# A hybrid decoder layer: operands made in pairs, the value unit moved back, and the convolution tail placed inside the output projection

## The chip, the cores and the metric

The kernel runs on one core of a Trainium2 chip. The metric is the device time of one execution in microseconds (us). Five engines work beside each other, each on its own queue: TensorE (PE: matmuls, and PEld: its weight loads), VectorE (DVE), ScalarE (ACT), GpSimd (POOL) and SyncE (SP), which issues most of the DMA transfers.

## The reference

One decoder layer over 2048 tokens of 1024 channels, in float32. A joint projection gives queries, keys and values for sliding-window attention, and the input of a gated convolution group; both outputs are joined and projected, and a SwiGLU feed-forward part follows. Cut to what matters:

```python
hn = rms_norm(x, mix_pre_g)
proj = hn @ w_in                       # q (8 heads), k and v (2 heads each), a and gate
attn = sliding_window_attention(q, k, v, attn_sinks, rel_bias)   # window 128, T5 bias, sinks
g = a * sigmoid(gate)                  # 512 channels
g = causal_depthwise_conv(g, conv_dw, width=31) + conv_dw_b
conv = silu(layer_norm(g, conv_ln_g, conv_ln_b)) @ w_conv_pw
h = x + rms_norm(concat([attn, conv]) @ w_out, mix_post_g)
hn = rms_norm(h, ffn_pre_g)
out = h + rms_norm((silu(hn @ w_gate) * (hn @ w_up)) @ w_down, ffn_post_g)
```

## The kernel before

The 2048 tokens are worked in four tiles of 512 (tile 0 to tile 3). Every float32 matmul operand is split into a high part (a copy rounded for the matmul, made by ACT) and a low part (the difference, made by DVE), and each product is three matmuls: high by high, high by low, low by high.

**A0 to A3 (`stage_a`)** project one token tile each: 14 units of 128 output channels, 24 matmuls each. Units 0 to 7 are the gates and inputs of the convolution group; then come K (unit 8), V (unit 9) and four query blocks q0 to q3. Results lie in four PSUM banks named `mm` until ACT or DVE copies or splits them. K goes to `kz`, V is transposed on PE and copied to `vtok`, the queries go to four `ql` tiles. `kz`, `vtok` and `ql` exist once, so a tile's K, V and queries overwrite what the attention of the tile before still reads. After each unit `step(i)` runs a hook, if there is one. The hooks prepare the next tile: `h1` loads its x, `h0` reads rows of x for the row norms, `h2` and `h3` make and spread the row scale (`gb`), and `h4` and `h5` each make four of the eight `hn` operands (`split_x`: a scaled product on DVE, a copy on ACT, a subtraction on DVE).

**B0 to B3 (`stage_b`)** are the attention of a tile, four blocks of 128 queries. `front(b)` makes the scores (PE from `ql` and `kz`, then masking, bias and maximum on DVE, exponentials on ACT); `back(b)` scales them, transposes them and makes the weighted sum with `vtok`. The order is front 0, front 1, back 0, front 2, back 1, front 3, back 2, back 3. They use three banks named `tr`.

**C0 to C3** are the convolution: 31 taps a block on DVE (`stage_taps`, tile `fc`), and a tail (`stage_tail`, `conv_tail`) that transposes, normalises over the channels, transposes back and applies the swish. The tail writes four 128x512 blocks to `mixT` in memory, as the attention does with its own four. **J** multiplies the pointwise convolution weights into the output weights. **W0 to W3 (`stage_w`)** read `mixT` for a tile, two channel blocks at a time (`gi` = 0 to 3; 0 and 1 are attention, 2 and 3 convolution), split them and multiply by the output weights; `norm_w` follows. **H, F and G** are the feed-forward part: sums of operands, up and gate products, down products.

The order of the work is written by generators. A main generator yields a cost after each piece; each yield pumps the lanes (`lb` attention, `lc` taps, `lw` output projections, `ld` join and tails of tiles 0 and 1, `lh` and others), which emit pieces at a set rate per unit of main cost. `lane.until(name)` emits the rest of a named item at once. A planner then orders the instructions of each engine by priority, which follows the order of emission (the taps stand back a little), and by when its own timeline has them ready. In tile 0 and tile 1 the hooks before are:

```python
hooks = {2: h1, 4: h0, 8: h2, 10: h3, 11: h4, 12: h5}   # t == 0
hooks = {0: h1, 2: h0, 7: h2, 9: h3, 10: h4, 11: h5}    # t == 1
```

Ahead of K, `before_kv()` emits all that is left of the attention of the tile before. Tiles 2 and 3 have their tails and output projections in lane `lw`, which runs beside the first down projection (G0): C2, W2, C3 (once tile 3's taps are done), W3.

Of the kernel before, what the change touches and what calls it, by code (L numbers as in the profile page):

```python
# [12 lines left out]
F32 = mybir.dt.float32  # L13
# [5 lines left out]
ALU = mybir.AluOpType  # L19
# [18 lines left out]
def layer_kernel(ctx, tc, x, xT, cols, rows, sinks, relb, onehot, w_in, w_four, w_pw, w_out, w_gate, w_up, w_down, out):  # L38
# [22 lines left out]
    def f2(tag, shape=(P, T)):  # L61
        return t_(tag, shape)
# [263 lines left out]
            hn.append(hk)  # L326
        return hn

    def stage_a(t, hn, before_kv, hooks, post=None):
        L = f"A{t}"  # L330
        lab[0] = L
        rb = None
# [54 lines left out]
        for c in range(4):  # L387
# [13 lines left out]
            half.send(proj(2 * c + 1, tr if post and c == 2 else mm))  # L401
            yield 5.2
            step(2 * c + 1)
        before_kv()
        lab[0] = L
        ok = proj(8)
        if t:
# [6 lines left out]
        vtt(kz[:, 1, P:], ok, kz[:, 0, P:].bitcast(F32), ALU.subtract)  # L414
        yield 5.2
        step(8)
        ov = proj(9)
        vt = f2("fa")
        if post:
            vtt(vt, ov, rb, ALU.mult)  # L420
        else:
            act(vt, ov, AF.Copy)
        yield 5.2
        step(9)
        q = []
        for i in range(4):
            oq = proj(10 + i)
            if i == 0:
                pv = mm()
                for s in range(4):  # L430
                    nc.tensor.transpose(pv[:, s * P : (s + 1) * P], vt[:, s * P : (s + 1) * P], ident)
                if t:
                    nc.vector.tensor_copy(vtok[:, 0], vtok[:, 4])
                nc.vector.tensor_copy(vtok[:, 1:5].rearrange("p a b -> p (a b)"), pv)
            qi = hl("ql")
            if post:
                qt = f2("fa")
                stt(qt, oq, 0.125, rb, ALU.mult, ALU.mult)
                act(qi[:, 0], qt, AF.Copy)
                vtt(qi[:, 1], qt, qi[:, 0].bitcast(F32), ALU.subtract)  # L440
            else:
                act(qi[:, 0], oq, AF.Copy, scale=0.125)
                stt(qi[:, 1], oq, 0.125, qi[:, 0].bitcast(F32), ALU.mult, ALU.subtract)
            q.append(qi)
            yield 5.2
            step(10 + i)
        qs[t] = q

    done_ = []
# [1 line left out]
    def stage_b(t):  # L451
# [115 lines left out]
            yield 1.8  # L567

        live = {}
        for b in range(5):  # L570
            if b < 4:
                yield from front(b)
            else:
                yield YC
            if b:
                yield from back(b - 1)

    def conv_in(t, c):
        g = t_("glu", (P, 576))[:, 0 : HALO + T]
# [29 lines left out]
            nc.sync.dma_start(y_scr[c, :, t * T : (t + 1) * T], y)  # L609
            yield 0.68  # L610

    def stage_tail(t):
        L = f"C{t}"
        lab[0] = L
        yt = t_("yt", (P, 4, 4 * P))
        ycs = []
        turn = turner(yt, ycs)
        for c in range(4):
            lab[0] = L
            y = f2("fc")  # L620
            nc.sync.dma_start(y, y_scr[c, :, t * T : (t + 1) * T])
            ycs.append(y)
            turn(c)
            yield 0.5
        yield from conv_tail(t, yt)

    def conv_tail(t, yt):
        L = f"C{t}"
        lab[0] = L
        mv = sm(8).rearrange("p (s a) -> p s a", a=2)  # L630
        for s in range(4):
            st = sm(6)
            nc.vector.bn_stats(st, yt[:, s])
            nc.vector.bn_aggr(mv[:, s], st)
        r = rsqrt(mv[:, :, 1], 4, 1.0)
        nmr = sm(4)
        stt(nmr, mv[:, :, 0], -1.0, r, ALU.mult, ALU.mult)
        yield YL if t < 2 else YL2
        lab[0] = L
        for s in range(4):  # L640
            act(yt[:, s], yt[:, s], AF.Identity, scale=r[:, s : s + 1], bias=nmr[:, s : s + 1])
        for c in range(4):
            b = ct()
            for s in range(4):
                nc.tensor.transpose(b[:, s * P : (s + 1) * P], yt[:, s, c * P : (c + 1) * P], ident)
            th = f2("fc")
            act(th, b, AF.Tanh, scale=lnh[:, c : c + 1], bias=lnh[:, 4 + c : 5 + c])
            v = f2("fc")
            act(v, b, AF.Identity, scale=ln_g[:, c : c + 1], bias=ln_b[:, c : c + 1])
            stt(v, th, 1.0, v, ALU.add, ALU.mult)  # L650
            nc.sync.dma_start(mixT[4 + c, :, t * T : (t + 1) * T], v)
            yield 2
            lab[0] = L

# [108 lines left out]
    def stage_w(w, spill, G, atag, htag, mtag, bank_of, norm=None):  # L763
        L = f"W{w}"
        lab[0] = L
        acc = [f4(atag) for _ in range(4)]

        def acts(gi, ms=None):
            aa = []
            for m in ms or load(gi):  # L770
                a = hl(htag)
                act(a[:, 0], m, AF.Copy)
                vtt(a[:, 1], m, a[:, 0].bitcast(F32), ALU.subtract)
                aa.append([a])
            return aa

        stage = spare_tile() if w == 1 else None

# [12 lines left out]
            lab[0] = L  # L791
        nxt = acts(0, first)
        for gi in range(KC // G):
            aa = nxt
            for n in range(2):
                lab[0] = L
                if n == 0 and gi + 1 < KC // G:
                    if w < 2 and G * gi + G == 4:
                        ld.until(f"C{w}")
                        lab[0] = L  # L800
                    rows_next = load(gi + 1)
                if n == 1 and gi + 1 < KC // G:
# [5 lines left out]
        tail = norm_w(w, spill, acc, mtag, gb)  # L808
        if norm:
            norm(tail)  # L810
        else:
            yield from tail

    def norm_w(w, spill, acc, mtag, gb):
        L = f"W{w}"
# [640 lines left out]
    for t in range(NT):  # L1456
        hooks = {}
        if t + 1 < NT:
# [7 lines left out]
            def h4(t=t + 1):  # L1466
                hn_a[t] = split_x(t, xa[t][0], xa[t][2], range(4))

            def h5(t=t + 1):
                hn_a[t] += split_x(t, xa[t][0], xa[t][2], range(4, KC))  # L1470

            def h0(t=t + 1):
                row_norms([t] if t == 1 else [2, 3], "p" if t == 1 else "hl")
# [3 lines left out]
                next(xa[t][2])  # L1477

            if t == 0:
                hooks = {2: h1, 4: h0, 8: h2, 10: h3, 11: h4, 12: h5}  # L1480
            elif t == 1:
                hooks = {0: h1, 2: h0, 7: h2, 9: h3, 10: h4, 11: h5}
            else:
                hooks = {H1: h1, H2: h2, H3: h3, H4: h4}
        run(mark(stage_a(t, hn_a[t], (lambda: lb.until(f"B{t-1}")) if t else (lambda: None), hooks,
                         None if t else norm_x(0, x0, sum_squares(0, x0))), f"A{t}"))
        lb.add(f"B{t}", stage_b(t))
        if t == 2:
            hn_a[t + 1] += split_x(t + 1, xa[t + 1][0], xa[t + 1][2], range(4, KC))
    lw.until("W0")  # L1490
# [14 lines left out]
    lc.until("T2")  # L1505
    lc.rates["T3"] = RC3
    ws, ops = (2, 3), {}
    lw.add("C2", stage_tail(2))
    lw.add("W2", stage_w(2, True, 2, "mid", "ql", "at", tr))
    lw.add("C3", stage_tail(3), lambda: since(lc, "T3", CS))  # L1510
    lw.add("W3", stage_w(3, True, 2, "mid", "ql", "at", tr, norm=lambda g: lw.add("N3", g)))
    lw.add("B11.2", stage_h_plain(ws, ops, "B11", 0))
    run(stage_p2((0, 1), mids[0], td))
    lw.until("N3")
# [70 lines left out]
```

## Time and profile before

| | |
|---|---|
| three timed runs, median (lowest to highest) | 1944.02 us (1936.79 to 1946.71) |
| the profiled execution, its own time | 1941.57 us |
| its span, first to last instruction | 1939.8 us |
| granted TensorE clock, mean | 0.993 |
| DMA traffic | 443.55 MB, mean 229 GB/s |

A row of the timeline begins with the start and the length in us, then the engine, the line, the operation and "output<-inputs". A tile's name carries the stage after an @: `mm@A` is an `mm` bank used by an A stage, `ql@W` a `ql` tile used by W. Most DVE instructions have the line of a helper, L85. In brackets stand the idle time of the engine before the row's first instruction and what ended it. In a table by stage each engine has its busy time and, in brackets, its number of instructions.

### The profile page before, as it was taken

What the parts mean: (1) busy time and instruction counts of PE and PEld (TensorE: products, weight loads), DVE (VectorE), ACT (ScalarE), POOL (GpSimd) and SP (SyncE); (2) the same over time, 40 slices, a digit from 0 to 9 for tenths busy, and PEclk for the clock granted to TensorE, in tenths of its full rate; (3) what the DMA queues carried; (4) which work ended last, traced back from release to release, by engine and by line L of the source; (5) the groups of instructions that cost most, each with busy time, mean ns of one, the idle gap of its engine ahead of it and who ended that gap; (6) DMA issues with size and microseconds to landing.
All of it is one profiled execution on the core that took longest, in us unless ns stands there. A gap on an engine that the chain in (4) does not pass through costs nothing.

```text
span 1939.8 us, 26752 instructions
## 1 busy us (share of the span) xinstructions
PE 1896.2 (98%) x8714; PEld 1537.5 (79%) x8714; DVE 1488.1 (77%) x2760; ACT 968.7 (50%) x1911; POOL 209.5 (11%) x311
## 2 busy tenths in 40 slices
PE   9998999999999999999999999999999999999998
PEld 7876776777678888877888788878888888888886
DVE  6998999988785999988988775778666665455557
ACT  5454444656667534333445466576533443345443
POOL 2010011221010000000000010010032332311000
PEclk9999999999999999999999999999999999999999
DMA  9876756678868776688397779589644442376654
GB/s 330 297 276 194 254 162 192 203 236 310 260 213 292 232 250 224 222 279 275 126 320 227 258 267 321 184 313 355 211 163 154 163 158 101 131 247 190 211 191 156
DMA packets 230011, 443.55 MB, mean 229 GB/s; under 512 B 22984, under 2 KB 49008, under 8 KB 229872
## 3 DMA queue, kind: packets, MB, share of 16 engines
q1 hardware_dynamic: 208560, 407.24, 63.1%
q10 hardware_dynamic: 19392, 28.32, 4.0%
q0 software_dynamic: 1920, 6.29, 0.8%
q8 instruction: 68, 1.11, 0.2%
q14 instruction: 71, 0.58, 0.1%
HBM read 320.64 MB, written 121.12 MB: 228 GB/s over the span
## 4 chain that ended last, share of the span: by engine, by line
PE 70%; DVE 16%; DMA 9%; issue 2%; ACT 2%; POOL 1%; SPq 0%; DVEq 0%; ACTq 0%; POOLq 0%
PE mm@F L108 37%; PE mm@G L108 19%; DVE fc@C L85 7%; PE mm@A L108 4%; PE tr@W L108 4%; PE mm@W L108 3%; PE tr@B L108 1%; DMA glu@C<-glu_scr 1%; DMA mixT<-fc@C 1%; DMA td<-fc@G 1%; DVE x@A L85 1%; DMA p@X<-w_four 1%; DMA p@A<-x 1%; DVE p@B L490 1%; DMA mids<-fa@F 1%
## 5 line engine op out<-in xcount | busy, mean ns | idle before, releaser
L85 DVE SCALAR_TENSOR_TENSOR fc@C<-glu@C,colt,fc@C 128x512 f32<-128x512 f32 x480 | 351.5, 751 | 1.7
L108 PE MATMUL mm@F<-hl@H,w@F 128*128 128x512 f32 x1056 | 254.3, 389 | 0.0
L108 PEld LDWEIGHTS mm@F<-hl@H,w@F 128*128 128x128 f32 x1056 | 197.9, 188 | 41.0
L108 PE MATMUL mm@G<-hl@G,hl@G 128*128 128x512 f32 x924 | 224.8, 393 | 2.6 <-DVE x@G L85 1.8
L864 ACT ACTIVATE w@F<-chl@F 128x512 fp32r<-128x512 f32 x220 | 135.5, 625 | 144.4 <-PE mm@F L108 138.6
L108 PEld LDWEIGHTS mm@G<-hl@G,hl@G 128*128 128x128 f32 x924 | 172.3, 188 | 39.0 <-ACT hl@G L864 3.4
L108 PE MATMUL mm@G<-w@G,hl@G 128*128 128x512 f32 x876 | 199.5, 389 | 0.0
L108 PE MATMUL mm@A<-hl@A,w@A 128*128 128x512 f32 x792 | 191.5, 394 | 1.2 <-DVE w@A L85 1.2
L108 PEld LDWEIGHTS mm@G<-w@G,hl@G 128*128 128x128 f32 x876 | 164.5, 188 | 34.1
L108 PEld LDWEIGHTS mm@A<-hl@A,w@A 128*128 128x128 f32 x792 | 147.4, 188 | 34.1 <-issue 1.7
L85 DVE TENSOR_TENSOR w@F<-chl@F,w@F 128x512 fp32r<-128x512 f32 x198 | 147.1, 747 | 35.7 <-ACT w@F L864 35.2
L108 PE MATMUL mm@F<-mid@H,w@F 128*128 128x512 f32 x528 | 131.7, 392 | 2.9 <-DVE fa@F L85 2.9
L108 PE MATMUL mm@F<-ql@H,w@F 128*128 128x512 f32 x528 | 130.2, 391 | 2.0 <-ACT w@F L864 1.6
L108 PE MATMUL mm@F<-p@H,w@F 128*128 128x512 f32 x528 | 129.0, 389 | 0.0
L108 PE MATMUL mm@F<-x@H,w@F 128*128 128x512 f32 x528 | 128.0, 391 | 0.0
L108 PEld LDWEIGHTS mm@F<-mid@H,w@F 128*128 128x128 f32 x528 | 99.6, 189 | 24.0 <-DVE fa@F L85 3.3
L108 PEld LDWEIGHTS mm@F<-ql@H,w@F 128*128 128x128 f32 x528 | 98.5, 188 | 23.3 <-ACT w@F L864 2.2
L108 PEld LDWEIGHTS mm@F<-x@H,w@F 128*128 128x128 f32 x528 | 98.7, 188 | 22.0 <-DVE sm@B L85 0.8
L108 PEld LDWEIGHTS mm@F<-p@H,w@F 128*128 128x128 f32 x528 | 99.1, 188 | 20.7 <-ACT at@F L1122 0.2
L85 DVE TENSOR_TENSOR w@G<-raw@G,w@G 128x512 fp32r<-128x512 f32 x73 | 50.4, 691 | 67.5 <-ACT w@G L864 66.6
L108 PE MATMUL mm@W<-w@W,hl@W 128*128 128x512 f32 x384 | 97.9, 401 | 4.2 <-ACT mid@W L745 1.9
L133 ACT ACTIVATE w@A<-raw@A 128x512 fp32r<-128x512 f32 x104 | 63.5, 625 | 75.1 <-PE mm@A L108 43.6
(310 smaller groups left out, 3194.1 us busy)
## 6 DMA issues: line engine op xcount, KB each, us to landing
mids<-fa@F SPq DMA_DIRECT2D x154, 256.0 KB, 2.7
raw@A<-w_in SPq DMA_DIRECT2D x52, 512.0 KB, 4.7
w@A<-lo_in SPq DMA_DIRECT2D x84, 256.0 KB, 3.8
fc@G<-mids SPq DMA_DIRECT2D x77, 256.0 KB, 3.4
fa@G<-mids SPq DMA_DIRECT2D x75, 256.0 KB, 5.1
w@W<-lo_out SPq DMA_DIRECT2D x48, 256.0 KB, 5.0
chl@F<-w_gate SPq DMA_DIRECT2D x22, 512.0 KB, 4.0
raw@F<-w_gate SPq DMA_DIRECT2D x22, 512.0 KB, 3.9
```

The source lines that it names most:

```text
L85: r = op(*args, **kw)
L108: r = nc.tensor.matmul(*args, **kw)
L133: act(w[:, 0], raw, AF.Copy)
L490: read = nc.vector.tensor_tensor_reduce(out=pr[:, h], in0=os[g][:, j, P:], in1=bias[0][:, h], op0=ALU.add, op1=ALU.max, scale=1.0, scalar=NEG,
L864: act(w[:, 0], x, AF.Copy)
```

## The change

Five edits. In `stage_a` the order of the last six units becomes K, q0, q1, q2, V, q3, and V's transposes follow q3's matmuls. The attention is handed over as two items: S (all fronts, and backs 0 and 1), emitted to its end ahead of K, and B (backs 2 and 3), emitted to its end after V's unit, ahead of q3. In tiles 0 and 1 the eight operands of the next tile are made two at a time over four units, by `pair_of`, and the hooks ahead of them are earlier. In W2 and W3 the tail is started by `stage_w` itself, pauses after its statistics, and goes on after the attention half; its results are split into operands at once and are neither written to `mixT` nor read from it. C2 and C3 are no longer items of lane `lw`.

```diff
-    def stage_a(t, hn, before_kv, hooks, post=None):
+    def stage_a(t, hn, done_with, hooks, post=None):
...
-        before_kv()
+        done_with("S")
         lab[0] = L
         ok = proj(8)
...
-        ov = proj(9)
-        vt = f2("fa")
-        if post:
-            vtt(vt, ov, rb, ALU.mult)
-        else:
-            act(vt, ov, AF.Copy)
-        yield 5.2
-        step(9)
         q = []
         for i in range(4):
+            if i == 3:
+                ov = proj(9)
+                vt = f2("fa")
+                if post:
+                    vtt(vt, ov, rb, ALU.mult)
+                else:
+                    act(vt, ov, AF.Copy)
+                yield 5.2
+                step(12)
+                done_with("B")
+                lab[0] = L
             oq = proj(10 + i)
-            if i == 0:
+            if i == 3:
                 pv = mm()
...
-            step(10 + i)
+            step(9 + i if i < 3 else 13)
...
-        for b in range(5):
-            if b < 4:
+        def scores():
+            for b in range(4):
                 yield from front(b)
-            else:
-                yield YC
-            if b:
-                yield from back(b - 1)
+                if 0 < b < 3:
+                    yield from back(b - 1)
+
+        def rest():
+            yield from back(2)
+            yield YC
+            yield from back(3)
+
+        return scores(), rest()
...
-            nc.sync.dma_start(mixT[4 + c, :, t * T : (t + 1) * T], v)
+            if sink:
+                sink(v)
+            else:
+                nc.sync.dma_start(mixT[4 + c, :, t * T : (t + 1) * T], v)
...
+        def operand(m):
+            a = hl(htag)
+            act(a[:, 0], m, AF.Copy)
+            vtt(a[:, 1], m, a[:, 0].bitcast(F32), ALU.subtract)
+            return [a]
+
         def acts(gi, ms=None):
...
+            return [operand(m) for m in ms or load(gi)]
+
+        conv = []
+        tail = stage_tail(w, lambda v: conv.append(operand(v))) if w > 1 else ()
+        for y in tail:
+            if y == YL2:
+                break
+            yield y
+        lab[0] = L
...
         for gi in range(KC // G):
-            aa = nxt
+            if w > 1 and G * gi == 4:
+                yield from tail
+                lab[0] = L
+            aa = nxt if w < 2 or G * gi < 4 else conv[G * gi - 4 : G * gi - 4 + G]
...
-            def h5(t=t + 1):
-                hn_a[t] += split_x(t, xa[t][0], xa[t][2], range(4, KC))
+            def pair_of(i, t=t + 1):
+                hn_a.setdefault(t, [])
+                hn_a[t] += split_x(t, xa[t][0], xa[t][2], range(2 * i, 2 * i + 2))
...
-                hooks = {2: h1, 4: h0, 8: h2, 10: h3, 11: h4, 12: h5}
+                hooks = {2: h1, 4: h0, 7: h2, 8: h3}
             elif t == 1:
-                hooks = {0: h1, 2: h0, 7: h2, 9: h3, 10: h4, 11: h5}
+                hooks = {0: h1, 1: h0, 5: h2, 7: h3}
             else:
                 hooks = {H1: h1, H2: h2, H3: h3, H4: h4}
-        run(mark(stage_a(t, hn_a[t], (lambda: lb.until(f"B{t-1}")) if t else (lambda: None), hooks,
+            if t < 2:
+                hooks.update({(9 if t == 0 else 8) + i: lambda i=i, f=pair_of: f(i) for i in range(4)})
+        run(mark(stage_a(t, hn_a[t], (lambda n: lb.until(f"{n}{t-1}")) if t else (lambda n: None), hooks,
...
-        lb.add(f"B{t}", stage_b(t))
+        for n, part in zip((f"S{t}", f"B{t}"), stage_b(t)):
+            lb.add(n, part)
...
-    lw.add("C2", stage_tail(2))
     lw.add("W2", stage_w(2, True, 2, "mid", "ql", "at", tr))
-    lw.add("C3", stage_tail(3), lambda: since(lc, "T3", CS))
-    lw.add("W3", stage_w(3, True, 2, "mid", "ql", "at", tr, norm=lambda g: lw.add("N3", g)))
+    lw.add("W3", stage_w(3, True, 2, "mid", "ql", "at", tr, norm=lambda g: lw.add("N3", g)),
+           lambda: since(lc, "T3", CS))
```

H4 is step 11; with the new order that is the unit of q2 in tile 2 (before, q1), in both cases the fourth of the last six.

More of the change, by code (lines that the diff above doesn't have):

```diff
@@ L610, in stage_taps, with stage_tail @@
             yield 0.68
-    def stage_tail(t):
+    def stage_tail(t, sink=None):
         L = f"C{t}"
@@ L624, in stage_tail, with conv_tail @@
             yield 0.5
-        yield from conv_tail(t, yt)
-    def conv_tail(t, yt):
+        yield from conv_tail(t, yt, sink)
+    def conv_tail(t, yt, sink):
         L = f"C{t}"
@@ L793, in stage_w @@
         for gi in range(KC // G):
-            aa = nxt
+            if w > 1 and G * gi == 4:
+                yield from tail
+                lab[0] = L
+            aa = nxt if w < 2 or G * gi < 4 else conv[G * gi - 4 : G * gi - 4 + G]
             for n in range(2):
                 lab[0] = L
-                if n == 0 and gi + 1 < KC // G:
+                more = gi + 1 < KC // G and (w < 2 or G * gi + G < 4)
+                if n == 0 and more:
                     if w < 2 and G * gi + G == 4:
@@ L801, in stage_w @@
                     rows_next = load(gi + 1)
-                if n == 1 and gi + 1 < KC // G:
+                if n == 1 and more:
                     nxt = acts(gi + 1, rows_next)
@@ L807, in stage_w @@
                 yield from block_half(acc, list(zip(aa, ws)), n, gi == 0, L, bank_of)
-        tail = norm_w(w, spill, acc, mtag, gb)
+        last = norm_w(w, spill, acc, mtag, gb)
         if norm:
-            norm(tail)
+            norm(last)
         else:
-            yield from tail
+            yield from last
     def norm_w(w, spill, acc, mtag, gb):
```

7 lines of the change are left out of this document (removed).

## The prediction

> **What bounds the kernel now.** I read the page's head first, then the waits of the matmul engine, then the busy time by stage, and last the timeline around the longest waits. The head says which engine sets the time; the stage table (length, then busy time and count of PE, PEld, DVE, ACT, POOL, then granted clock, DMA share, GB/s) says where that engine is not full.
>
> ```profile
> span 1939.8 us, 26752 instructions
> PE 1896.2 (98%) x8714; PEld 1537.5 (79%) x8714; DVE 1488.1 (77%) x2760; ACT 968.7 (50%) x1911; POOL 209.5 (11%) x311
> ...
> 90.00:195.00 105.00, 94.64 (x476) 73.71 (x475) 89.14 (x220) 52.39 (x135) 8.94 (x15) 0.97 0.73 244
> 195.00:292.00 97.00, 97.00 (x483) 74.22 (x481) 90.16 (x198) 43.80 (x120) 8.10 (x7) 1.00 0.65 207
> 292.00:387.00 95.00, 88.57 (x472) 67.89 (x470) 92.46 (x216) 54.12 (x129) 15.74 (x28) 0.98 0.61 195
> 387.00:545.00 158.00, 154.39 (x792) 118.11 (x790) 131.23 (x313) 96.22 (x221) 24.94 (x54) 0.99 0.77 257
> ...
> 1000.00:1296.00 296.00, 290.04 (x1311) 238.38 (x1310) 221.12 (x389) 173.45 (x307) 15.29 (x60) 0.99 0.78 266
> ```
>
> PE is busy for 1896.2 of 1939.8 us, so every gain must come out of 43.6 us of idle PE and of stretches with a clock below 1.00; the change neither adds nor removes a matmul. The five stages shown are those that the edits reach. The first is the projection of token tile 1 (A1) beside the attention of tile 0 (B0): PE idles 105 - 94.64 = 10.4 us, at clock 0.97. The second, mostly A2 with B1, has no idle PE. The third (start of A3) has 6.4 us, the fourth 3.6 us, the fifth (down projection beside the output projections W2 and W3) 6.0 us. Idle time in all of them is 26.4 us: the ceiling, before clock losses. DVE is busy 89.14 of 105, 90.16 of 97 and 92.46 of 95 us in the first three; there DVE is nearly a second bound, so where its instructions stand in its queue matters.
>
> ```profile
> PE mm@A L108 <- DVE ql@A L85: 4.7, 1, 4.7
> PE tr@B L108 <- DVE vtok L433: 3.3, 1, 3.3
> PE tr@W L108 <- ACT ql@W L772: 3.3, 2, 2.5
> ```
>
> These are single stalls, not a pattern of the loop (total, times, longest). The longest, 4.7 us on the split of a query block, stands in A1. The third is W waiting for operands of the convolution half.
>
> **The operands of tile 2 in pairs.** The timeline of the last third of A1:
>
> ```profile
> 159.11 0.59 ACT L310 ACTIVATE gb@A<-mm@A 128x512 f32<-128x512 f32 x1
> ...
> 164.80 1.41 DVE L85 SCALAR_TENSOR_TENSOR x@A<-x@A,colt,gb@A 128x512 f32<-128x512 f32 x2
> 166.78 4.06 DVE L85 SCALAR_TENSOR_TENSOR x@A<-x@A,colt,gb@A 128x512 f32<-128x512 f32 x6
> 171.94 2.48 DVE L85 TENSOR_TENSOR hl@A<-x@A,hl@A 128x512 fp32r<-128x512 f32 x4
> 174.17 0.98 PE L108 MATMUL mm@A<-chl@A,w@A 128*128 128x512 f32 x3
> 175.01 2.48 DVE L85 TENSOR_TENSOR hl@A<-x@A,hl@A 128x512 fp32r<-128x512 f32 x4
> 175.34 1.09 ACT L442 ACTIVATE ql@A<-mm@A 128x512 fp32r<-128x512 f32 x2 [0.45 <-PE mm@A L108]
> 178.36 0.75 DVE L487 COPY_PREDICATED tr@B<-upper,tr@B 128x256 f32<-128x256 int8 x2
> 179.14 1.23 DVE L85 SCALAR_TENSOR_TENSOR ql@A<-mm@A,ql@A 128x512 fp32r<-128x512 f32 x2
> 179.82 5.49 PE L108 MATMUL mm@A<-mid@A,w@A 128*128 128x512 f32 x12 [4.67 <-DVE ql@A L85]
> 187.35 0.97 PE L108 MATMUL tr@B<-kz,ql@A 64*128 64x256 f32 x12
> 188.39 0.60 ACT L413 ACTIVATE kz<-mm@A 128x512 fp32r<-128x512 f32 x1 [2.41 <-PE tr@B L108]
> 189.45 2.91 PE L108 MATMUL mm@A<-mid@A,w@A 128*128 128x512 f32 x12
> ```
>
> Reading: the row scale lands in gb at 159.11, and from 164.80 to 177.49 DVE makes all eight operands of the next tile almost without a break: 1.41 + 4.06 + 2.48 + 2.48 = 10.43 us. ACT has its half of q0 and q1 ready by 176.43, but DVE's half starts at 179.14, behind that block and the masking of B0's scores. PE's four "mm" banks are full (K, which waits for the last score to 188.39; V's transposes; q0; q1), so PE idles 4.67 us. Then it starts slowly: 12 matmuls take 5.49 us, where the same 12 take 2.91 at 189.45, so 2.58 us more go to the clock (0.97 in the stage row). The place costs 7.25 us.
>
> The change issues the same 8 DVE pairs as two after each of K, q0, q1 and q2: 10.43 / 4 = 2.61 us a unit, instead of four after q0 and four after q1, and its scale is asked for two units earlier (steps 5 and 7, were 7 and 9). No block of over about 2.6 us then stands ahead of a q split. DVE's half can follow ACT's at once, at 176.43 instead of 179.14: 2.71 us less, and with under 2 us of idle left no slow restart, 5.29 us in all. The rest depends on the score before it, which lies in the same DVE queue behind the same block. I take the whole 7.25 us; the bounds are 0 (if the planner packs them again) and 7.25. What is late next is B0's last score, which holds K's bank. For tile 1 the operands get the same spreading in A0, and no PE wait on them stands in the list: 0.
>
> [...]
>
> **K, three q units, V, the last q; scores apart from the rest.** The unit order changes, not the units. K and the q blocks overwrite what B's scores read; only V's copy overwrites what the remainder of B reads (its second half: two weighted sums). So the forced emission ahead of K shrinks to the scores, and the remainder is spread over K to q2. Nothing new is issued. How early that part was wanted, and how late it ran, shows in A2:
>
> ```profile
> 295.96 0.60 PE L431 MATMUL mm@A<-ident,fa@A 128*128 128x128 f32 x4
> ...
> 300.85 0.97 PE L108 MATMUL tr@B<-kz,ql@A 64*128 64x256 f32 x12
> ...
> 327.62 1.03 PE L108 MATMUL tr@B<-p@B,vtok 128*64 128x512 f32 x4
> ...
> 330.51 0.65 DVE L434 COPY vtok<-mm@A 128x512 f32<-128x512 f32 x1
> ```
>
> V's transposes lie in a bank from 295.96 to 331.16, 35 us, because the copy must follow B1's last weighted sum at 327.62; B1's last score ran at 300.85. The transposes now come three units later, at 97.00 / 14 = 6.9 us a unit, so that bank is held some 21 us less, while others are held as before: at the fifth unit after K's start, K, q0, q1 and q2 are held instead of K, V's transposes, q0 and q1. That is a trade of equals up to the last score, and a bank more after it. A2 has no idle PE to win. The 3.3 us wait named vtok in A3 is a queue of DVE work (92.46 of 95 us busy), which this does not shorten; tile 3's eight operands, too, keep their two blocks of four (the first after the fourth of the last six units, as before). I book for B0's own waits in A1,
>
> ```profile
> 154.87 0.97 PE L108 MATMUL tr@B<-kz,ql@A 64*128 64x256 f32 x12 [1.88 <-DVE sm@B L490]
> ...
> 171.39 1.08 PE L108 MATMUL tr@B<-p@B,vd@B 128*64 128x512 f32 x4 [1.68 <-POOL p@B L535]
> ```
>
> half of 1.88 + 1.68, 1.8 us gained (bounds 0 and 3.6). On SP's queue the eight row loads of A1 come one unit earlier, ahead of that unit's weights, beside the four x loads:
>
> ```profile
> hl@A<-x SPq DMA_DIRECT2D x8, 512.0 KB, 9.2
> ...
> 111.29 2.57 PE L108 MATMUL mm@A<-mid@A,w@A 128*128 128x512 f32 x10 [2.13 <-DMA w@A<-lo_in]
> ```
>
> 4 MB at the stage's 244 GB/s are 17 us of traffic moved by one unit, while the x buffers come free earlier. The weight wait of 2.13 us may go or double: 0, bounds -2.1 and +2.1.
>
> **The convolution tail inside W2 and W3.** Before, the tail writes its four blocks to memory and W reads them back:
>
> ```profile
> mixT<-fc@C SPq DMA_DIRECT2D x16, 256.0 KB, 4.9
> ...
> at@W<-mixT SPq DMA_DIRECT2D x12, 256.0 KB, 4.5
> ...
> 1059.10 0.32 SPq L651 DMA_DIRECT2D mixT<-fc@C  x1
> 1063.94 0.32 SPq L784 DMA_DIRECT2D at@W<-mixT  x1
> 1068.55 0.63 ACT L772 ACTIVATE ql@W<-at@W 128x512 fp32r<-128x512 f32 x1 [2.79 <-DMA at@W<-mixT]
> 1069.23 2.88 PE L108 MATMUL tr@W<-w@W,ql@W 128*128 128x512 f32 x6 [2.54 <-ACT ql@W L772]
> ...
> 1078.04 1.52 PE L108 MATMUL tr@W<-w@W,ql@W 128*128 128x512 f32 x6
> ```
>
> Eight of the 16 writes and eight reads go, 4 MB; at 266 GB/s in that stage 16 us of traffic, hidden. Visible is one round trip, 1059.10 to 1068.53, with PE idle 2.54 us at its end, and a slow restart: 2.88 against 1.52 for six matmuls. Together 3.90 us. ACT's and DVE's splits stay, eight and eight. The tail now sits between the halves of each W, so W's matmuls wait for its chain directly: transposes, two ACT passes, a DVE product, the split. Queued behind such a matmul on PE are the down projection's own. Per W this costs 0 to 2.5 us (2.54 is the nearest row, the same wait with a slower source); I take 0.5 each, as W's first half runs ahead of it: +1.0. The pause between a tail's statistics and its use goes, so both W end earlier in the stage; with only 6.0 us idle there, 0.
>
> [...]
>
> **The sum.** -7.25 - 1.8 - 3.90 + 1.0 = -11.95 us. The profiled execution took 1941.57 us (span 1939.8), which gives 1929.6. The three timed runs have median 1944.02, 2.45 us higher, so against them it would be 1932.1. I say 1931 us, between the two.
>
> **The rivals.** (1) *The planner undoes it.* Emission order is only a priority: instructions start when the planner's own timeline calls them ready, and DVE stays nearly full (90.16 of 97 us). The eight operands bunch elsewhere, or a new stall of the same size replaces the 7.25 us. For it: B1's late second half shows how far emission and execution differ. Against it: the scale arrives two units earlier, so work is ready earlier. Then only the W place counts: 1941.57 - 3.9 = 1937.7, or 1940 against the median.
>
> (2) *The scores become the bound (slower).* K, q0, q1 and q2 hold all four banks, and V cannot start until a score lets one go. Decisive is whether B's last score runs within four units of K's start. In A1 it ran at 187.35, 7.5 us after PE resumed at 179.82. If the earlier operand work and the spread remainder hold the scores back, PE stands until then: 7.5 us more in A1 with the present stall kept, and in A2 the same 7.5 plus 2.58 of clock. That is 17.6 - 3.9 = +13.7: 1955.3. A3 is safe:
>
> ```profile
> 419.35 0.97 PE L108 MATMUL tr@B<-kz,ql@A 64*128 64x256 f32 x12
> ...
> 459.47 0.60 PE L431 MATMUL mm@A<-ident,fa@A 128*128 128x128 f32 x4
> ```
>
> its last score is 40 us ahead of V. For this rival: A1's stall already is a full set of banks. Against it: the scores are emitted as before and lose the 10.43 us block that stood in front of them.
>
> [...]
>
> **How the numbers follow.** A measurement of this kernel can tell about 0.5% (9.7 us) from no change: faster is below 1934.3, slower above 1953.7. The forecast gets 0.55 (0.41 below 1934.3, 0.14 above); rival 1 gets 0.22 (0.03 faster, 0.17 same, 0.02 slower); rival 2 gets 0.23 (0.06 same, where the lateness is smaller than priced, 0.17 slower). Sums: faster 0.44, same 0.37, slower 0.19. The range: down to 1917, where the third and fourth stages give back another 10.0 us of idle, and B0's waits (1.8 more) and the weight wait (2.1) go entirely; up to 1955, rival 2. The forecast's own range is 1922 to 1938.
>
> **What would show it.** In A1: no PE wait on ql, no run of eight x or hl operands on DVE, the stage's clock at 1.00 and idle PE about 2 us or less. In A2 and A3: V's transposes held clearly under 35 us, and the 3.3 us wait still there or moved. In W: no reads of mixT for the convolution half, no tr wait over 1 us on ql. [...]

## The result, and the profile after

In 18 runs each, the changed kernel has a median of 1936.79 us and the kernel before 1941.76 us: ratio 0.9977, 95% interval 0.9968 to 0.9987. That is 5.0 us where 12 were forecast: the right side and inside the range, but less than half the size. The profile's head and the same stage table as before (length, then busy time and count of PE, PEld, DVE, ACT, POOL, then granted clock, DMA share, GB/s):

```profile
span 1934.7 us, 26719 instructions
PE 1897.4 (98%) x8714; PEld 1535.7 (79%) x8714; DVE 1492.1 (77%) x2760; ACT 970.4 (50%) x1911; POOL 211.5 (11%) x311
```

```profile
90.00:195.00 105.00, 105.00 (x532) 82.05 (x531) 101.68 (x243) 62.52 (x158) 10.53 (x18) 1.00 0.79 267
195.00:292.00 97.00, 97.00 (x499) 75.16 (x498) 93.70 (x218) 43.04 (x122) 7.84 (x6) 1.00 0.61 196
292.00:387.00 95.00, 86.76 (x444) 66.09 (x443) 86.94 (x199) 53.39 (x129) 17.74 (x30) 0.96 0.66 206
387.00:545.00 158.00, 154.27 (x784) 118.55 (x783) 128.78 (x309) 99.41 (x224) 25.07 (x58) 0.98 0.74 249
545.00:1000.00 455.00, 444.71 (x1961) 362.48 (x1960) 388.15 (x621) 206.61 (x373) 6.04 (x20) 1.00 0.72 242
1000.00:1296.00 296.00, 293.92 (x1331) 240.51 (x1330) 225.13 (x400) 179.50 (x319) 19.58 (x64) 0.99 0.77 258
```

The first row is the forecast come true and more: A1 has no idle PE (10.4 us before) and its clock went from 0.97 to 1.00. The second is as full as before. The third and fourth rows go the other way: idle 8.2 + 3.7 = 12.0 us where it was 6.4 + 3.6 = 10.0, at clocks of 0.96 and 0.98 where they were 0.98 and 0.99, which is, as an estimate from these rows, another 95 x 0.02 + 158 x 0.01 = 3.5 us. By these rows the two stages are worse by 5.5 us. But the rows are fixed stretches of time, and the changed kernel is some 11 us further on in them; counted by its work, in the table below, the stretch from A2 to W1 is longer by 0.4 us only. The waits of PE, longest first, name the places:

```profile
PE mm@W L108 <- ACT hl@W L782: 5.1, 1, 5.1
PE mm@F L108 <- DVE fa@F L85: 3.5, 2, 2.7
PE mm@F L108 <- ACT w@F L888: 3.3, 2, 2.1
PE mm@G L108 <- ACT hl@G L888: 3.0, 2, 2.4
PE ct@C L602 <- DMA fc@C<-y_scr: 2.9, 2, 2.5
PE mm@W L108 <- ACT mid@W L757: 2.8, 1, 2.8
...
PE tr@W L108 <- ACT ql@W L782: 0.4, 1, 0.4
```

The waits on ql of A1 and on vtok of A3 are gone from the list, the one on ql of W fell from 3.3 to 0.4. New at the head stands W0's wait for its first operands. Stage lengths, in us, in one profiled execution each (A1 and G0 end at the start of their last matmul, the others at the first matmul of the next stage; the last two kernels are explained with the last experiments):

| kernel | to A1's end | A2 to W1 | F0 | G0 | F2 | rest | span |
|---|---|---|---|---|---|---|---|
| before | 195.2 | 350.0 | 433.2 | 317.8 | 421.7 | 221.9 | 1939.8 |
| after | 184.0 | 350.4 | 439.8 | 318.2 | 420.1 | 222.2 | 1934.7 |
| after, two waits taken away (k9) | 185.0 | 346.7 | 432.6 | 318.8 | 420.1 | 222.3 | 1925.5 |
| before, the same two edits (k12) | 194.3 | 348.1 | 435.1 | 316.2 | 420.9 | 222.1 | 1936.7 |

A1 ends 11.2 us earlier, and F0 seems to take 6.6 us back. The experiments show that F0's 6.6 us lie within the scatter of single executions, and look for the loss ahead of F0.

### The profile page after: what moved, and what is told of

It reads as the page before. It is cut to its first block, busy times and chain, and to the rows that moved or that the text cites. A ratio compares the mean times of both kernels' runs of the same rounds, so it can differ in the third digit from the quotient of the medians.

```text
span 1934.7 us, 26719 instructions
## 1 busy us (share of the span) xinstructions
PE 1897.4 (98%) x8714; PEld 1535.7 (79%) x8714; DVE 1492.1 (77%) x2760; ACT 970.4 (50%) x1911; POOL 211.5 (11%) x311
## 4 chain that ended last, share of the span: by engine, by line
PE 67%; DVE 16%; DMA 11%; issue 3%; ACT 1%; POOL 1%; SPq 0%; DVEq 0%; ACTq 0%; POOLq 0%
PE mm@F L108 35%; PE mm@G L108 18%; DVE fc@C L85 7%; PE tr@W L108 4%; PE mm@A L108 4%; PE mm@W L108 3%; PE tr@B L108 1%; DMA glu@C<-glu_scr 1%; DVE w@F L85 1%; DMA mids<-fa@F 1%; DMA chl@F<-w_gate 1%; DVE fa@F L85 1%; DVE p@B L493 1%; DMA wx@G<-w_down 1%; DMA fa@G<-mids 1%
## 5 line engine op out<-in xcount | busy, mean ns | idle before, releaser
L85 DVE SCALAR_TENSOR_TENSOR fc@C<-glu@C,colt,fc@C 128x512 f32<-128x512 f32 x480 | 353.3, 753 | 1.9
L85 DVE TENSOR_TENSOR w@F<-chl@F,w@F 128x512 fp32r<-128x512 f32 x198 | 144.2, 732 | 35.3 <-ACT w@F L888 34.9
L108 PEld LDWEIGHTS mm@F<-mid@H,w@F 128*128 128x128 f32 x528 | 99.4, 189 | 25.1 <-DVE fa@F L85 4.4
L108 PE MATMUL mm@W<-w@W,hl@W 128*128 128x512 f32 x384 | 102.0, 411 | 8.2 <-ACT hl@W L782 5.1
L85 DVE TENSOR_TENSOR w@G<-raw@G,w@G 128x512 fp32r<-128x512 f32 x73 | 51.3, 703 | 67.0 <-ACT w@G L888 66.0
```

The source lines that it names most:

```text
L85: r = op(*args, **kw)
L108: r = nc.tensor.matmul(*args, **kw)
```

## The experiments

### The parts alone

The first kernel has the change in stage A and W as before; the second the reverse. The third leaves the units and the attention as before and has only the new hooks (pairs, and the scale two units earlier); the fourth has the new unit order and the split attention with the old hooks (two blocks of four).

```diff
 # e1_stage_a_only: the changed kernel, with the kernel before's
-    def stage_tail(t, sink=None): ...   # and the new conv half of stage_w
+    lw.add("C2", stage_tail(2)) ... lw.add("C3", stage_tail(3), ...)
 # e2_tail_in_w_only: the kernel before, with the changed kernel's stage_tail, conv_tail, stage_w, lw.add
 # e3_pairs_only: the kernel before, and
-                hooks = {2: h1, 4: h0, 8: h2, 10: h3, 11: h4, 12: h5}
+                hooks = {2: h1, 4: h0, 7: h2, 8: h3}    # and pair_of(i) at 9 + i
 # e4_order_only: the changed kernel's stage_a and stage_b, W as before, and
+                hooks = {2: h1, 4: h0, 8: h2, 10: h3, 11: h4, 12: h5}
```

> All edits of the projection stages (units reordered, scores split off, operands in pairs), the tails and output projections of tiles 2 and 3 as before. Its order of instructions is that of the changed kernel up to the middle of the first down projection (G0). Theory 1 (the projections gain 10.8 us, and what the later stages gave back in the one profile is chance): 9 to 11 us under the kernel before. Theory 2 (the stages behind give back part of it every time, in A3 and in F0): 4 to 6 us under it, with F0 longer than before by 3 us or more in this profile too.

> Only the tail inside W2 and W3; everything up to G0 is in the order of the kernel before. Theory 1 and 2 alike, from the two profiles (G0 is 317.8 us long before and 318.2 after): 0 us, within 1.5. The prediction's own step (3.9 us for the wait on the read-back operands, less 1.0): 2.9 us under the kernel before.

> Only the operands of tiles 1 and 2 in pairs with the earlier hooks; K, V, q0 to q3 and the hand-over of the attention as before. If the pairs carry the gain in A1 (as the prediction had it): no PE wait on ql in A1, A1 shorter by 7 us or more, and a time like that of all stage A edits. If the new order carries it: A1 keeps a wait of 3 us or more and the time is within 2 us of the kernel before.

> Only the new order of the units and the split hand-over; the eight operands stay in two blocks of four, at the old steps. If the pairs carry the gain: the 10 us block of DVE and a PE wait of 3 us or more in A1 stay, time within 2 us of the kernel before. If the order carries it: A1 without the wait, 5 us or more under the kernel before.

| kernel | median us | before | ratio (95%) | A1 long |
|---|---|---|---|---|
| e1, stage A | 1937.64 | 1939.47 | 0.9986 (0.9972 to 1.0000) | 92.6 |
| e2, tail in W | 1939.26 | 1939.47 | 1.0006 (0.9991 to 1.0021) | 107.0 |
| e3, pairs | 1950.43 | 1939.47 | 1.0059 (1.0043 to 1.0075) | 99.4 |
| e4, order | 1938.06 | 1939.47 | 0.9993 (0.9981 to 1.0006) | 94.3 |

A1 took 105.3 us before and 92.5 after. The order alone brings 11.0 us of these 12.8, the new hooks alone 5.9. e1, with A1 as short as in the full change, gains 2.7 us by its ratio (0 to 5.4): nearer to its second theory, but without that theory's longer F0 (432.3 us, before 433.2). The timeline of e4, the same place as in the prediction:

```profile
162.08 5.38 DVE L85 SCALAR_TENSOR_TENSOR x@A<-x@A,colt,gb@A 128x512 f32<-128x512 f32 x8
172.05 4.42 PE L108 MATMUL mm@A<-mid@A,w@A 128*128 128x512 f32 x12 [2.94 <-DVE ql@A L85]
...
296.81 6.28 PE L108 MATMUL mm@A<-hl@A,w@A 128*128 128x512 f32 x17 [4.97 <-DVE ql@A L85]
```

and of e3:

```profile
145.73 5.38 DVE L85 SCALAR_TENSOR_TENSOR x@A<-x@A,colt,gb@A 128x512 f32<-128x512 f32 x8
175.62 5.49 PE L108 MATMUL mm@A<-mid@A,w@A 128*128 128x512 f32 x12 [3.17 <-DVE ql@A L85]
...
335.75 1.65 PE L108 MATMUL tr@B<-kz,ql@A 64*128 64x256 f32 x12 [5.71 <-DVE sm@B L490]
```

In both, the planner runs all eight scaled products in one block, whether they were issued as fours or as pairs. In e4 the block stands about where it stood, and a wait of 2.94 us on ql remains. In e3 it comes 19 us earlier (164.80 before), and a wait on ql of 3.17 us remains all the same. Only both together leave none. And in both a new wait of about 5 us appears a stage or two later, with a slow restart (17 matmuls in 6.28 us in e4, where 24 took 5.75 at 475.12; 12 in 1.65 in e3, where the same 12 took 0.97 in the kernel before); e3 is the slowest kernel of all, with its A1 6 us shorter than before. A stage that gets faster is no gain by itself here.

The tail in W, for which the forecast had 2.9 us, shows nothing: between 1.7 us gained and 4.1 lost.

### Is F0 the place that takes it back?

F0 has the same order of instructions on PE, DVE, ACT and SP in the kernel before, in the changed one, in e1 and in e2. In it, SP issues stores to `mids` and the reads of `keeps` on one queue, and ACT waits for these reads (64.7 us in the changed kernel's profile, 47.3 before). So the first theory was that the changed state at F0's start makes these reads late. One run repeats the changed kernel; two move the reads to POOL's queue, in the changed kernel and in the one before; one moves the stores of `td`.

```diff
 # k2_keeps_pool_after and k3_keeps_pool_before
-                nc.sync.dma_start(kept[m], keep[m])
+                (nc.sync if ws[0] else nc.gpsimd).dma_start(kept[m], keep[m])
 # k4_td_pool_after
-            nc.sync.dma_start(td[to, pr], o)
+            nc.gpsimd.dma_start(td[to, pr], o)
```

> The changed kernel once more, unaltered, for a second profile and a second timing beside the kernels below. Theory 1 (the stages behind the projections only scatter: F0 has the same order of instructions in both kernels): 9 us under the kernel before when more runs are counted, with F0 (from its first product on the H operands in p to the first down product) anywhere from 302 to 310 us. Theory 2 (the give-back comes back every time): 4 to 6 us under it, as the first time.

> The changed kernel with F0's loads of its kept products issued from the POOL queue, so that they no longer stand behind stores on SP's queue that wait for DVE. If ACT's wait for these loads (64.7 us in the changed kernel's profile, 44.1 in the one with the stage A edits alone) sets F0's length: the wait falls under 25 us, F0 to 302 us or less, the time 4 us or more under the changed kernel. If F0's length comes from elsewhere (DVE, the clock): the wait falls and the time stays within 2 us.

> The same queue change on the kernel before. If F0's loads hid the gain of A1: this kernel gains less than the changed one does by the queue change, and the two with the queue change differ by 9 us. If the gain is lost elsewhere: they differ by 4 to 6 us, as without it.

> The changed kernel with the 44 stores of summed down weights issued from the POOL queue; the loads stay on SP. If it is these stores on SP's queue that hold up the loads behind them: ACT's wait for the kept products halves and F0 falls to 303 us or less, 3 us or more under the changed kernel. If the loads are late for traffic, not for their place in the queue: no difference within 2 us.

| kernel | median us | before | ratio (95%) | F0 after its first part |
|---|---|---|---|---|
| k1, the change again | 1935.87 | 1940.68 | 0.9981 (0.9964 to 0.9997) | 305.6 |
| k2, reads on POOL, after | 1934.35 | 1940.68 | 0.9968 (0.9951 to 0.9984) | 306.6 |
| k3, reads on POOL, before | 1941.58 | 1940.68 | 1.0004 (0.9990 to 1.0019) | 307.8 |
| k4, td on POOL, after | 1936.00 | 1940.68 | 0.9976 (0.9959 to 0.9994) | 305.3 |

The theory fell. The reads' queue makes no difference that can be told, and on POOL's queue the wait did not go either. ACT's wait on `keeps` was 36.6 us in k1, 50.2 in k2 and 44.1 in e1, in no relation to F0's length: with the same order of work that part took 305.0 (before), 309.7 (after), 305.6 (k1), 302.1 (e1) and 307.8 (e2). The 4.7 us between the first two are no more than this scatter. k1 also repeats the result: 4.8 us.

### The waits of the new plan in A3, W0 and W1

What does repeat in e1, k1, k2, k4 and the changed kernel are three waits: 5.07 to 5.10 us, 1.8 to 3.0 us and 2.6 to 4.9 us. The timeline of the changed kernel around the first two, with the queue of SP (its rows are issues) ahead of them:

```profile
315.24 0.33 SPq L143 DMA_DIRECT2D raw@A<-w_in  x1
321.99 0.32 SPq L618 DMA_DIRECT2D y_scr<-fc@C  x1
...
322.83 0.93 SPq L804 DMA_DIRECT2D fa@W<-mixT  x2
326.72 1.27 ACT L782 ACTIVATE hl@W<-fa@W 128x512 fp32r<-128x512 f32 x2 [3.91 <-DMA fa@W<-mixT]
327.40 0.80 PE L108 MATMUL mm@W<-w@W,hl@W 128*128 128x512 f32 x1 [5.08 <-ACT hl@W L782]
...
380.27 0.63 PE L602 MATMUL ct@C<-ident,fc@C 128*128 128x128 f32 x4 [2.49 <-DMA fc@C<-y_scr]
```

The first is W0's wait for its operands (327.40), the second the convolution's for a read of `y_scr` (380.27). SP stands from 315.57 to 321.99 in front of the taps' store to `y_scr`, which waits for DVE (`SPq L618 <- DVE fc@C L85: 6.3, 1, 6.3` in the queue's own waits), and W0's two reads stand behind it. They are issued at 322.83, reach ACT's split at 326.72, and PE waits 5.08 us. Before, the same place had 3.30 us on vtok and 1.42 us on hl, 4.72 us together: one pair of waits went and another of nearly the same size took its place. The second wait was 0.8 us before, the third 1.89 us. The third wait is W1's, behind W0's norm:

```profile
460.56 0.62 POOL L159 TENSOR_TENSOR sm@W<-sm@W 128x4 f32<-128x4 f32 x1 [15.32 <-DVE sm@W L85]
461.25 0.71 POOL L160 TENSOR_TENSOR sm@W<-sm@W,sm@W 128x4 f32<-128x4 f32 x1
...
467.10 0.20 POOL L162 TENSOR_TENSOR sm@W<-sm@W,sm@W 128x4 f32<-128x4 f32 x1
467.33 2.19 ACT L873 ACTIVATE x@W<-x@W,sm@W 128x1024 f32<-128x1024 f32 x2 [5.43 <-POOL sm@W L162]
...
474.70 7.25 PE L108 MATMUL mm@W<-w@W,hl@W 128*128 128x512 f32 x18 [2.81 <-ACT mid@W L757]
```

POOL works through twelve tiny instructions of a reciprocal root in 6.7 us, ACT waits 5.43 us for it at the head of its queue, and ACT's copies of W1's banks (`mid`) come late; PE waits 2.81 us and then needs 7.25 us for 18 matmuls. Four experiments, all on the changed kernel (the kernel before had 1938.84 us beside them):

```diff
 # k5_w0_loads_pool
-                nc.sync.dma_start(ms[-1], mixT[c, :, w * T : (w + 1) * T])
+                (nc.gpsimd if w == 0 else nc.sync).dma_start(ms[-1], mixT[c, :, w * T : (w + 1) * T])
 # k6_taps_store_pool
-            nc.sync.dma_start(y_scr[c, :, t * T : (t + 1) * T], y)
+            nc.gpsimd.dma_start(y_scr[c, :, t * T : (t + 1) * T], y)
 # k8_w0_norm_dve (the last argument puts the root on POOL)
-        r2 = rsqrt(ssq2, 4, D, w < 3)
+        r2 = rsqrt(ssq2, 4, D, 0 < w < 3)
 # k9_both: k5 and k8
```

> The changed kernel with W0's loads from mixT on the POOL queue. In five profiles with the changed stage A, PE waits 5.07 to 5.10 us at the start of W0 for these operands; on SP their loads stand behind a taps' store that waits for DVE. If that place in the queue is the cause: the wait falls under 1 us, the stretch from the end of A1 to F0 shortens by 4 us or more, and the time is 3 us or more under the changed kernel. If the loads are late by their own latency or by B's results: the wait stays at 4 to 5 us.

> The changed kernel with the taps' stores to y_scr on the POOL queue, the loads left on SP. The same cause taken away from the other side: if the store on SP is it, both the 5.1 us wait of W0 and the 1.8 to 3.0 us wait of the second tail on its load shrink, 4 us or more under the changed kernel. Against it: POOL then waits for the taps itself, and the attention's selections behind it come later; then new waits on POOL appear and the time is the same or longer.

> The changed kernel with the second reciprocal root of W0's norm made on DVE instead of POOL, where its 12 small steps take 6.7 us while ACT waits 5.43 us for them and PE then 2.6 to 4.9 us for a bank. If that chain is the cause of the wait at 476: the wait falls under 1 us and the slow restart (18 matmuls in 5.8 to 7.3 us) goes, 3 us or more under the changed kernel. If not: the wait stays.

> W0's loads on POOL's queue and its second reciprocal root on DVE, together. If the gain of A1 is given back at these two waits: the two savings add, 6 us or more under the changed kernel and 10 us or more under the kernel before. If what is saved there turns up as a wait further on: no more than the better one of the two alone.

| kernel | median us | ratio (95%) | W0's first wait | at W1 |
|---|---|---|---|---|
| after | 1936.79 | 0.9977 (0.9968 to 0.9987) | 5.08 | 2.81, then 18 matmuls in 7.25 |
| k5 | 1928.59 | 0.9940 (0.9920 to 0.9960) | 1.06 | 2.04, then 18 in 4.38 |
| k6 | 1931.32 | 0.9957 (0.9942 to 0.9972) | 5.14 | 3.65 (on ql), then 18 in 7.03 |
| k8 | 1930.87 | 0.9958 (0.9943 to 0.9973) | 4.96 | none |
| k9 | 1927.23 | 0.9935 (0.9915 to 0.9955) | 1.05 | none |

In k5 the reads are issued nine us earlier and the wait all but goes; its timeline:

```profile
313.57 1.08 POOL L804 DMA_DIRECT2D fa@W<-mixT  x2
325.67 0.50 PE L108 MATMUL mm@W<-w@W,hl@W 128*128 128x512 f32 x1 [1.06 <-ACT hl@W L782]
```

In k8 the wait at W1 goes, with the slow restart (29 matmuls in 6.91 us):

```profile
475.80 6.91 PE L108 MATMUL mm@W<-w@W,hl@W 128*128 128x512 f32 x29
```

k6 is a miss with a lesson. With the store off SP the wait stayed 5.14 us: SP now stood 5.8 us in front of another read of `mixT`, which waits for the attention's store, and W0's two reads were again issued late (322.28). Another waiting DMA ahead of the reads on the same queue (5.8 us) did the same as that store (6.3).

```profile
SPq L804 <- DMA mixT<-at@B: 5.8, 1, 5.8
...
317.99 0.80 SPq L804 DMA_DIRECT2D mb@J<-mixT  x2
...
322.28 0.90 SPq L804 DMA_DIRECT2D fa@W<-mixT  x2
```

The time fell nevertheless (0.9957 against the changed kernel's 0.9977), and which part of k6 brought that stays open: the wait that was to go did not. The edit also made the planner order the work anew (PE's order differs from the changed kernel's in 1040 of 8714 places), so a new plan may be worth as much as one of these waits; no run tells the two apart.

k9 is the best of all, though not the sum of k5 and k8. A new wait took part of it, in its timeline:

```profile
324.65 0.50 PE L108 MATMUL mm@W<-w@W,hl@W 128*128 128x512 f32 x1 [1.05 <-ACT hl@W L782]
342.64 2.93 PE L108 MATMUL mm@W<-w@W,hl@W 128*128 128x512 f32 x6 [5.65 <-ACT x@W L757]
```

### Do these waits belong to the change?

The same two edits could be improvements of any version. So the last three kernels are the kernel before with k5's edit, with k8's, and with both.

> The kernel before, with only W0's reads of mixT issued from POOL's queue instead of SP's. On the changed kernel the same edit took the wait on W0's first operands from 5.08 to 1.06 us and the ratio from 0.9977 to 0.994, some 7 us. Theory 'given back by the change': the kernel before has 3.30 us on DVE's vtok and only 1.42 us on hl at this place, so at most 1.4 us can go here: ratio 0.9993 to 1.000, and the 3.30 us wait stays. Rival 'an improvement of its own, which has nothing to do with the change': the same 5 to 7 us, ratio 0.9965 to 0.9975.

> The kernel before, with only W0's second reciprocal root on DVE instead of POOL. On the changed kernel it removed a 2.8 us wait on mid and a slow restart (18 matmuls 7.25 to 4.42 us) and the ratio went from 0.9977 to 0.9958, some 4 us. Theory 'given back by the change': the kernel before waits 1.89 us there and restarts at once (17 matmuls 4.31 us), so at most 1.9 us: ratio 0.999 to 1.000. Rival 'an improvement of its own': some 4 us, ratio 0.998 or less.

> The kernel before, with both edits. On the changed kernel both gave 0.9935 in place of 0.9977, 8 us more. Theory 'given back by the change': at most 1.4 + 1.9 = 3.3 us, ratio 0.9983 to 1.000, so that the change is worth 8 us or more on top of the two edits. Rival 'an improvement of its own': 8 us, ratio about 0.996, and the change is worth its 5 us with the edits or without.

| edit | on the kernel before | on the changed kernel |
|---|---|---|
| none | 1 | 0.9977 (0.9968 to 0.9987) |
| W0's reads off SP | 1.0022 (1.0007 to 1.0038), k10 | 0.9940 (0.9920 to 0.9960) |
| W0's root off POOL | 1.0000 (0.9986 to 1.0014), k11 | 0.9958 (0.9943 to 0.9973) |
| both | 0.9998 (0.9982 to 1.0013), k12 | 0.9935 (0.9915 to 0.9955) |

Medians were 1943.38, 1938.65 and 1939.37 us, beside 1938.90 for the kernel before. On it the edits bring nothing; on the changed kernel both bring 0.0042, some 8 us. So by the timed runs the waits were mostly a price of the new plan, not an old fault. In k10 the wait that was there stays, in another place in the queue, and the one at W1 grows from 1.89 to 2.74 us, with a slow restart (24 matmuls in 7.29 us, 5.89 before):

```profile
336.64 1.65 PE L108 MATMUL tr@B<-kz,ql@A 64*128 64x256 f32 x12 [4.73 <-DVE vtok L433]
...
486.53 7.29 PE L108 MATMUL mm@W<-w@W,hl@W 128*128 128x512 f32 x24 [2.74 <-ACT mid@W L745]
```

There the bound at A3's start is V's copy on DVE, so earlier reads only shift the wait (3.30 before). The change took that bound away, and SP's queue came next. With the two waits away, the change is worth 0.9935 against 0.9998: about 12 us. That is the size that was forecast, but not by the forecast's terms, as the next section shows.

The profiles place less than half of the 8 us. From A1's end to F0 the new plan takes 350.1 to 353.3 us in five profiles (after, e1, k1, k2, k4; mean 351.5) and the old one 349.0 to 350.0 in three (before, e2, k3; mean 349.5). With the edits it is 345.1 (k5), 349.1 (k8) and 346.7 (k9) on the changed kernel, and 352.2 (k10), 348.0 (k11) and 348.1 (k12) on the kernel before. Both edits thus save 4.8 us there on the new plan and 1.4 on the old one; where the rest of the 8 us lies is not shown. Each edit also changes the planner's order elsewhere, as k6 showed, and k10 is 4.3 us slower than the kernel before, so single effects of some 4 us can be the new order's. And the changed kernel itself was not timed in the round of k5 to k9; their ratios have the kernel before in common.

## Why the prediction was right and wrong

**A1: right in size, wrong in mechanism.** Forecast were 7.25 + 1.8 = 9.05 us, with the weight wait of 2.13 us as a bound. A1 starts 1.6 us later, lasts 12.8 us less and ends 11.2 us earlier. All of its PE waits went, with the slow restart: 7.25 + 1.88 + 1.68 + 2.13 = 12.9 us, where the sum had booked half of the middle two and nothing of the last. But the step "No block of over about 2.6 us then stands ahead of a q split" failed. The changed kernel's DVE timeline:

```profile
150.34 4.05 DVE L85 SCALAR_TENSOR_TENSOR x@A<-x@A,colt,gb@A 128x512 f32<-128x512 f32 x6
...
154.40 0.74 DVE L85 SCALAR_TENSOR_TENSOR x@A<-x@A,colt,gb@A 128x512 f32<-128x512 f32 x1
...
157.04 2.49 DVE L85 TENSOR_TENSOR hl@A<-x@A,hl@A 128x512 fp32r<-128x512 f32 x4
...
163.54 0.68 DVE L85 SCALAR_TENSOR_TENSOR ql@A<-mm@A,ql@A 128x512 fp32r<-128x512 f32 x1
```

The eight operands run together, as rival 1 said, but 14.5 us earlier than before (150.34 against 164.80), ahead of the q splits. Built with two blocks of four at the first two of these steps in place of four pairs, the changed kernel has the same order of instructions on every engine (it was not run): the pairs are no edit at all, the earlier hooks are. And e4 shows that V's move and the split attention, booked by me at 1.8 us for B0's waits, carry most: A1 was 94.3 us with them alone.

**V's bank: right.** V's transposes of A2 start at 305.48 and their copy ends at 311.57: 6.1 us instead of 35, in the changed kernel's timeline:

```profile
305.48 0.38 PE L434 MATMUL mm@A<-ident,fa@A 128*128 128x128 f32 x2
...
310.89 0.68 DVE L437 COPY vtok<-mm@A 128x512 f32<-128x512 f32 x1
```

The 3.3 us wait on vtok, which I said the change "does not shorten", went. It had hidden what came next.

**"A2 has no idle PE to win", A3 at nothing: the step that failed.** I asked what is late next only inside A1, and answered K's bank. Everything behind A1 was booked at its old waits. With work arriving some 11 us earlier, W0's reads met a store on SP, and W0's norm met its own root on POOL: three waits, of which the two on those queues cost some 8 us by the timed runs (k9 against the change, with k12 against the kernel before), and 3.4 us by the stage lengths of single profiles. Both queues were in the profile; the prediction looked at SP only for x loads and weights.

**The tail in W: too much, the second step that failed.** Forecast were 2.9 us, 3.90 for the round trip less 1.0. Its signs came as said: the reads of `mixT` for `at` fell from 12 to 4, the wait on ql from 3.3 to 0.4. In the row from 1000 us PE's idle time went down by 3.9 us, but G0 as a whole lasted 318.2 us where it had 317.8, and e2's ratio says 1.2 us lost, with 1.7 gained at the good end of its interval. Just ahead of that row the changed kernel has a wait of 2.41 us on hl of G; a kernel with the old tail has it too (3.3 us in k11), so it need not be the new tail's. Why the wait that went brought nothing stays open.

**The rivals.** Rival 2 (scores as the bound) did not occur: no PE wait on kz or on a bank in A1. Rival 1 gave 1940 us against the median shown, 3.9 us gained, for "a new stall of the same size": its number is nearest, and its bunching happened, but the new stalls stand two stages away and A1's is gone.

**The sum.** Of the 11.95 us, A1's 9.05 were there and more (11.2), the tail's 2.9 were not, and what stands behind A1, booked at nothing, took back most of the rest; 5.0 us were left. The time lies inside the forecast's range by the width of the range, not because the terms held.

**What stays open.** The mean stage lengths of the changed kernels' profiles would make the change worth some 3 us more than its timed runs; with single executions of one order 7 us apart in F0, that cannot be assigned.

## What to carry to other kernels

When a stall in the middle of a planned kernel goes, everything behind it runs against different partners: list for the next stages what stands at the head of each queue (here SP's store that waited 6.3 us for DVE, a root of 6.7 us on POOL, ACT 5.43 us behind it) and price what would be late if the work came that much earlier. To learn whether a wait belongs to a change, take it away in both versions; here the same two edits were worth 8 us on one and nothing on the other, though each edit also gave a new plan of the rest. And look at what the planner makes of an edit before crediting it: an edit that leaves every engine's order as it was cannot be the cause.

## What the hardware showed that I had not expected

**After gaps of 1.8 to 3 us some restarts were slow, and the gap's length did not decide which.** At W1 24 matmuls took 5.89 us after a gap of 1.89 us in the kernel before, and 7.36 after one of 1.79 in e2, which has the same order of work up to there. After 3.03 us in e4 nine matmuls took 2.25 (ten undisturbed ones at 389.93 took 2.43); the changed kernel's 18 after 2.81 took 7.25, against 4.38 after 2.04 in k5. At A1's weight wait ten took 2.57 after 2.13 (before) and 4.15 after 2.18 (e2). In W six took 2.88 after 2.54 (before) against 1.52 undisturbed. From before, e2 and e4 in this order:

```profile
485.85 5.89 PE L108 MATMUL mm@W<-w@W,hl@W 128*128 128x512 f32 x24 [1.89 <-ACT mid@W L745]
...
488.96 7.36 PE L108 MATMUL mm@W<-w@W,hl@W 128*128 128x512 f32 x24 [1.79 <-ACT mid@W L748]
...
337.05 0.51 PE L108 MATMUL mm@W<-w@W,hl@W 128*128 128x512 f32 x1 [3.03 <-ACT hl@W L781]
337.40 2.25 PE L108 MATMUL mm@A<-mid@A,w@A 128*128 128x512 f32 x9
```

The granted clock goes with them. In the kernel before it was 0.51 behind the 4.67 us gap of A1 (179.80 to 185.40) and 0.52 behind the 2.54 us gap of W (1069.20 to 1072.20), but 0.99 behind 2.13 (111.20 to 113.90) and 1.00 behind 1.89 (485.80 to 491.80); in the changed kernel it was 0.58 behind 2.81 (474.70 to 482.00). What decides between the two is not shown. The prediction's "with under 2 us of idle left no slow restart" fits the gap of 1.88 us in its own row at 154.87 (12 in 0.97 us), but it is not safe, by e2's 1.79. At W1 the changed kernel's gap of 2.81 us cost 2.8 + 2.9 us (18 matmuls in 7.25, in k5 4.38).

**POOL's tiny instructions took three times as long beside DVE's taps.** Those of W0's root (128x4) take 0.62 to 0.71 us up to 465.89 and 0.19 to 0.20 us from 465.98. DVE runs seven taps from 460.36 to 465.84, and then pauses:

```profile
460.36 5.48 DVE L85 SCALAR_TENSOR_TENSOR fc@C<-glu@C,colt,fc@C 128x512 f32<-128x512 f32 x7
...
465.98 0.20 POOL L162 TENSOR_TENSOR sm@W<-sm@W,sm@W 128x4 f32<-128x4 f32 x1
```

In the kernel before, other DVE instructions stand between the taps. Beside the split of a query block (479.34 to 480.02) and the masking of scores (480.60 to 481.35) POOL's instructions of the same root took 0.20 us, beside the taps that start at 479.94 and 481.26 they took 0.61 and 0.68. What makes them longer is not shown. The changed kernel's root took 6.7 us; with twelve starts 0.28 us apart, as the short ones have them, an estimate gives 12 x 0.28 = 3.4.
